# First norm's chain taken first, residual affine passes later, last down projection skewed by 14 rows

## The chip, the core and the metric

One core of one Trainium2 chip runs one launch. The metric is device time in microseconds (us): the median of three runs of the kernel before is 1265.94 us (1265.94 to 1266.82). The profiled execution took 1265.78 us; its span, from the first to the last instruction, is 1264.0 us. TensorE is PE (its weight loads PEld), VectorE is DVE, ScalarE is ACT, SyncE is SP; every load of this kernel is issued from SP's queue.

## The reference

One decoder layer on 256 tokens of width 2048, float32. It mixes tokens (mLSTM and HGRN2 heads, input and output projection), then runs a SwiGLU feed-forward of width 5632. Both sub-layers are modulated by six vectors `mod = silu(c) @ w_mod + b_mod`, and each ends in a residual and a layer norm:

```python
sh1, sc1, g1, sh2, sc2, g2 = jnp.split(mod[:, None, :], N_MOD, axis=-1)
u = x * (1.0 + sc1) + sh1
y = token_mixer(u, ...)                                   # ends with y @ w_out
x = layer_norm(ALPHA * x + (1.0 + g1) * y, ln1_g, ln1_b)  # the first norm
u = x * (1.0 + sc2) + sh2
y = (silu(u @ w_gate) * (u @ w_up)) @ w_down
x = layer_norm(ALPHA * x + (1.0 + g2) * y, ln2_g, ln2_b)  # the second norm
```

## The kernel before

**Split weights.** Each float32 product is made of three matmuls, high by high, high by low and low by high. A weight tile of 128x1024 (512 KB) is loaded by SP into `wr` (4 buffers), ACT copies it to the rounded high half `wh` (5 buffers), DVE subtracts to get the low half `wl` (5 buffers). `w1` (L706) does this, `three` (L718) the matmuls. The 256 tokens are two blocks of 128 rows, t0 and t1, which are the stationary operand; the weights stream past them, 512 columns a matmul.

**Modulation.** Each of 96 vectors `mod(j)` (L170) is a 1 MB load into `m` (2 buffers) and one DVE pass of 128x2048 (L174). Those with j of 48 to 79 (shift and scale of the second sub-layer) are wanted in four groups c, each of four j from 48 on and four from 64 on: `affine1(c)` turns them into the scale and bias columns `sc` with which `make_u2` makes the feed-forward's input `u2` for its k steps 4c to 4c+3. 34 of the 48 modulations of the output projection's stage are spread before it ends; the 14 left (`late`) are asked for by `some(2)` at each k step of the first feed-forward stage.

**Output projection and first norm.** `wo` is taken in two parts over four column groups c. In the last group the matmuls of t0 come first and those of t1 after them (`skew`). `resid` multiplies a bank by the gate (L732) and adds it to the residual `z` (L736), `stat` takes the statistics (L739). Then `norm1(t)`: aggregate (L743), two tiny ACT operations, four passes over z (L810). `turn` transposes z on PE (L817), `make_u2` scales the result on ACT, splits it on ACT and makes the low half on DVE (L838).

**Feed-forward.** `ffn_in((0, 1))` is the first stage: 16 k steps, each with two weight tiles (g = 0 and 1) and both token blocks, 24 matmuls a step. The affine passes that turn the normed z into the residual of the second sub-layer (`affine`, L922 and L923, with the vectors l1g and l1b loaded by `spill`, L847) are asked for in the later stages `up_to`. `down` is the down projection in two passes over four column groups; in the last group of the second pass the last 8 rows (four weight tiles) run first for t0 and then for t1. `finish(t)` is the second norm: statistics, then per quarter L978 and L979 and a store.

**What sets the order.** The program is traced once, and a scheduler orders each engine's instructions by priority, by what it reckons to be ready and by free buffers. `tc.high_priority(n)` raises what is traced inside it, `add_manual_dep` puts one instruction behind another of the same engine without a semaphore. On the chip each engine, and SP's queue, works its list strictly in order.

Of the kernel before, what the change touches and what calls it, by code (L numbers as in the profile page):

```python
# [3 lines left out]
F32 = mybir.dt.float32  # L4
F32R = mybir.dt.float32r
# [32 lines left out]
FIRST = 34  # L38
MIX = (("qk g i", "first"), ("v", "second"), ("o", "p last n"))
NATIVE = ((), ())  # L40
PRI = dict(w=400, e=0, m=-200)

PK = {}
_at = 0
# [35 lines left out]
def build(nc, tc, d):  # L80
    from contextlib import ExitStack

    with ExitStack() as ctx:
# [538 lines left out]
        def mods_some(a):  # L622
            credit[0] += a
            while credit[0] >= 1:
                credit[0] -= 1
                next(modq, 0)
# [77 lines left out]
                act(o[:, 512 * c : 512 * c + 512], bank, AF.Copy)  # L704
            return o

        def w1(src):
            cnt[0] += 1
            r = wr.tile([P, 1024], F32, tag="w", name=f"wr{cnt[0]}")
            nc.sync.dma_start(r, src)  # L710
            h = wh.tile([P, 1024], F32R, tag="h", name=f"wh{cnt[0]}")
            l = wl.tile([P, 1024], F32R, tag="l", name=f"wl{cnt[0]}")
            with tc.high_priority(PRI["w"]):
                act(h, r, AF.Copy)
                tt(l, r, h.bitcast(F32), ALU.subtract)  # L715
            return h, l

        def three(banks, h, l, a, b, first, last):  # L718
# [39 lines left out]
        for part in (1, 0):  # L758
            for c in range(4):
                if part:  # L760
                    banks[c] = [ps(), ps()]
                tiles = []
                skew = part == 0 and c == 3
                for p in range(4):
                    tiles.append(w1(d["wo"][16 * (1 - part) + 4 * c + p]))
                    mods_some(RATE[2])
                    if not skew:
                        for t in range(2):
                            for j in range(2):
                                k = 8 * part + 2 * p + j  # L770
                                w = slice(512 * j, 512 * j + 512)
                                three([banks[c][t]], tiles[-1][0][:, w], tiles[-1][1][:, w], half(yh, k, t), half(yl, k, t), part == 1 and k == 8, part == 0 and k == 7)
                if skew:
                    for t in range(2):
                        for p in range(4):
                            for j in range(2):
                                k = 2 * p + j
                                w = slice(512 * j, 512 * j + 512)
                                three([banks[c][t]], tiles[p][0][:, w], tiles[p][1][:, w], half(yh, k, t), half(yl, k, t), False, k == 7)
                if part == 0:  # L780
                    for t in range(2):
                        resid(t, c, banks[c][t], G1, ALPHA)
                        stat(t, c)
        run(modq)
        late = order2[FIRST:]

        def some(n):
            for _ in range(n):
                if late:
                    run(mod(late.pop(0)))  # L790

        def affine1(c):
            w = slice(4 * c, 4 * c + 4)
            tt(Ac[:, w], pc("l1g", 4 * c, 4), modc[:, 64 + 4 * c : 68 + 4 * c], ALU.mult)
            tt(Bc[:, w], pc("l1b", 4 * c, 4), modc[:, 64 + 4 * c : 68 + 4 * c], ALU.mult)
            tt(Bc[:, w], Bc[:, w], modc[:, 48 + 4 * c : 52 + 4 * c], ALU.add)

        affine1(0)
        affine1(1)
        u2h = [M(name="u2h", dt=F32R) for _ in range(4)]  # L800
        u2l = [M(name="u2l", dt=F32R) for _ in range(4)]

# [3 lines left out]
        def norm1(t):  # L806
            mu, rs = norm(t)
            for c in range(4):
                w = slice(512 * c, 512 * c + 512)
                ts(z[t][:, w], z[t][:, w], mu, rs, ALU.subtract, ALU.mult)  # L810

        zt = {}

        def turn(t, c):
            bank = ps()
            for j in range(4):
                nc.tensor.transpose(bank[:, P * j : P * j + P], z[t][:, 512 * c + P * j : 512 * c + P * j + P], ident)  # L817
            if c < 2:
                zt[t, c] = bank
                return  # L820
            if t == 0:
                zt[c] = M(name="zt")
            zt[t, c] = zt[c][:, 512 * t : 512 * t + 512]
            act(zt[t, c], bank, AF.Copy)

        def make_u2(t, c):
            u = S(512, "s5", bufs=CFG["s5"])
            for j in range(4):
                k = 4 * c + j
                w = slice(P * j, P * j + P)  # L830
                act(u[:, w], zt[t, c][:, w], AF.Identity, scale=Ac[:, k : k + 1], bias=Bc[:, k : k + 1])

            def part(x):
                return x[c].rearrange("p (k t) -> p k t", t=T)[:, :, t * P : t * P + P]
# [9 lines left out]

        def spill(name):
            o = A(name="bc")
            nc.sync.dma_start(o, d[name].broadcast_to([P, D]))  # L847
            return o

        def swi(g, t, gate, up):  # L850
# [28 lines left out]

            return bk, held, block  # L880

        norm1(0)
        for c in range(4):
            turn(0, c)
            if c < 2:
                make_u2(0, c)
        norm1(1)
        use_set(AF.Silu)
        tc.add_manual_dep(table["load"], table["var"].name, order, reason="table")
        bk, held, block = ffn_in((0, 1))  # L890
        for k in range(2):
            for g in range(2):
                held[k, g] = w1(d["wf"][g * KT + k])
            block(k, 0)
        for c in range(4):
            turn(1, c)
            if c < 2:
                make_u2(1, c)
        for k in range(2):
            block(k, 1)  # L900
        for k in range(2, KT):
# [17 lines left out]

        def affine(t, c):  # L920
            w = slice(512 * c, 512 * c + 512)
            stt(z[t][:, w], z[t][:, w], ALPHA, Ag[:, w], ALU.mult, ALU.mult)  # L922
            stt(z[t][:, w], Ab[:, w], ALPHA, z[t][:, w], ALU.mult, ALU.add)  # L923

        mods = list(range(80, 96))
# [20 lines left out]
        def down(k0, k1, G, last):  # L946
            for c in range(4):
                bk = [ps(), ps()]
                held = {}
                skew = 8 if last and c == 3 else 0  # L950

                def pair(k, t):
                    for j in range(2):
                        w = slice(512 * j, 512 * j + 512)
                        three([bk[t]], held[k][0][:, w], held[k][1][:, w], hslice(k + j, t, 0), hslice(k + j, t, 1), k + j == k0, k + j == k1 - 1)

                for k in range(k0, k1, 2):
                    held[k] = w1(d["wd"][22 * c + k // 2])
                    if k < k1 - skew:
                        for t in range(2):  # L960
                            pair(k, t)
                    if k == k0 + 4:
                        while pend:
                            flip(pend.pop(0))
                for t in range(2):
                    for k in range(k1 - skew, k1, 2):
                        pair(k, t)
                    resid(t, c, bk[t], G, None)
                    if last:
                        stat(t, c)  # L970
                        if c == 3:
                            finish(t)

        def finish(t):
            mu, rs = norm(t)
            for c in range(4):
                w = slice(512 * c, 512 * c + 512)
                stt(z[t][:, w], z[t][:, w], mu, Lg[:, w], ALU.subtract, ALU.mult)  # L978
                stt(z[t][:, w], z[t][:, w], rs, Lb[:, w], ALU.mult, ALU.add)  # L979
                nc.sync.dma_start(d["out"][t][:, w], z[t][:, w])  # L980
# [73 lines left out]
```

## Time and profile before

| | |
|---|---|
| median of 3 runs | 1265.94 us |
| profiled execution, its span | 1265.78 us, 1264.0 us |
| PE busy | 1212.8 us, 96% |
| DVE busy | 901.2 us, 71% |
| ACT busy | 591.7 us, 47% |
| DMA | 259 GB/s mean over the span, 285 to 341 GB/s in most slices of the first feed-forward stage |

The page cuts the span into 40 slices of 31.6 us. PE is full in all of them but the first (load and start), the 17th (505.6 to 537.2 us, the first norm, where the granted clock is 0.8 as well) and the last (the second norm). The waits of PE and the timelines of these two places show who was late there.

### The profile page before, as it was taken

Reading aid. Unit: us, or ns where it says so; the run is one execution under the profiler, and the core shown is the slowest. Engines: PE = TensorE matmul, PEld = TensorE weight load, DVE = VectorE, ACT = ScalarE, POOL = GpSimd, SP = SyncE. Lnnn points to the kernel's source line nnn. Section 1 sums busy time; section 2 is a strip of 40 time slices with the busy share of each in tenths; the row PEclk is TensorE's granted clock in tenths of the full one; section 3 lists DMA queues with packets and bytes.
Section 4 is the critical chain, followed back from the end, with each engine's and each line's share of the span. In section 5 each row is a group of like instructions: output and inputs, shape, how many; then the busy total and the mean of one; then the engine's idle time right before and its main releaser. Section 6 shows DMA issues by size and latency. Waiting matters only on the chain.

```text
span 1264.0 us, 17132 instructions
## 1 busy us (share of the span) xinstructions
PE 1212.8 (96%) x6706; PEld 1040.0 (82%) x6706; DVE 901.2 (71%) x979; ACT 591.7 (47%) x743; POOL 3.9 (0%) x13
## 2 busy tenths in 40 slices
PE   4899999999999999799999999999999999999995
PEld 4888899997889887688888888888888888888884
DVE  6778997999999979997877554455555445445655
ACT  4554454835664644644544444433344444434340
POOL 0000000000000000000000000000000000000000
PEclk9999999999999999899999999999999999999998
DMA  9998997857788989889998666666666666676661
GB/s 364 386 335 328 341 398 285 301 200 264 267 327 308 330 317 334 305 320 327 324 329 325 192 190 189 178 194 191 198 191 192 189 194 185 193 256 184 191 191 66
DMA packets 75968, 328.00 MB, mean 260 GB/s; under 512 B 8432, under 2 KB 8816, under 8 KB 62704
## 3 DMA queue, kind: packets, MB, share of 16 engines
q1 hardware_dynamic: 75888, 326.92, 74.9%
q8 instruction: 52, 0.85, 0.3%
q14 instruction: 28, 0.23, 0.0%
HBM read 324.79 MB, written 2.10 MB: 259 GB/s over the span
## 4 chain that ended last, share of the span: by engine, by line
PE 89%; DVE 5%; ACT 3%; issue 2%; DMA 1%; DVEq 0%; ACTq 0%
PE ps L722 21%; PE ps L725 21%; PE ps L721 21%; PE ps L251 5%; PE ps L249 5%; PE ps L250 5%; PE ps L260 2%; PE ps L261 2%; PE ps L262 2%; DVE m L174 2%; PE ps L447 1%; ACT wh L128 1%; DMA m<-in_wmod 1%; DVE wl L213 1%; PE ps L863 1%
## 5 line engine op out<-in xcount | busy, mean ns | idle before, releaser
L128 ACT ACTIVATE wh<-wr 128x1024 fp32r<-128x1024 f32 x408 | 431.1, 1059 | 550.8 <-PE ps L722 426.2
L715 DVE TENSOR_TENSOR wl<-wr,wh 128x1024 fp32r<-128x1024 f32 x296 | 360.6, 1224 | 283.7 <-ACT wh L128 280.4
L721 PE MATMUL ps<-wh,u2h 128*128 128x512 f32 x704 | 275.6, 392 | 0.3 <-ACT s L128 0.3
L722 PE MATMUL ps<-wh,u2l 128*128 128x512 f32 x704 | 273.7, 389 | 0.1
L174 DVE CUSTOM_DVE_ANT_0 m<-m,cb,init 128x2048 f32<-128x2048 f32 x96 | 225.1, 2346 | 22.3 <-DMA m<-in_wmod 22.0
L725 PE MATMUL ps<-wl,u2h 128*128 128x512 f32 x704 | 217.0, 389 | 0.0
L249 PE MATMUL ps<-uh,wh 128*128 128x256 f32 x640 | 184.4, 292 | 22.5 <-ACT wh L128 17.1
L250 PE MATMUL ps<-ul,wh 128*128 128x256 f32 x640 | 181.8, 286 | 0.0
L251 PE MATMUL ps<-uh,wl 128*128 128x256 f32 x640 | 180.3, 287 | 1.1 <-DVE wl L213 1.0
L721 PEld LDWEIGHTS ps<-wh,u2h 128*128 128x128 f32 x704 | 132.6, 188 | 28.9 <-ACT s L128 0.7
L722 PEld LDWEIGHTS ps<-wh,u2l 128*128 128x128 f32 x704 | 132.0, 188 | 28.0 <-DVE u2l L838 0.8
L725 PEld LDWEIGHTS ps<-wl,u2h 128*128 128x128 f32 x704 | 132.1, 188 | 27.6
L213 DVE TENSOR_TENSOR wl<-wr,wh 128x1024 fp32r<-128x1024 f32 x112 | 135.8, 1221 | 25.1 <-ACT wh L128 24.5
L249 PEld LDWEIGHTS ps<-uh,wh 128*128 128x128 f32 x640 | 123.6, 194 | 25.0 <-ACT wh L128 17.8
L721 PE MATMUL ps<-wh,hid 128*128 128x512 f32 x352 | 137.2, 390 | 0.0
L725 PE MATMUL ps<-wl,hid 128*128 128x512 f32 x352 | 137.0, 389 | 0.0
L722 PE MATMUL ps<-wh,hid 128*128 128x512 f32 x352 | 137.0, 389 | 0.0
L250 PEld LDWEIGHTS ps<-ul,wh 128*128 128x128 f32 x640 | 124.5, 195 | 1.3 <-issue 1.0
L251 PEld LDWEIGHTS ps<-uh,wl 128*128 128x128 f32 x640 | 123.2, 194 | 1.9 <-DVE wl L213 1.8
L725 PEld LDWEIGHTS ps<-wl,hid 128*128 128x128 f32 x352 | 66.1, 188 | 13.9
L721 PEld LDWEIGHTS ps<-wh,hid 128*128 128x128 f32 x352 | 66.1, 188 | 13.6
L722 PEld LDWEIGHTS ps<-wh,hid 128*128 128x128 f32 x352 | 66.1, 188 | 13.6
(179 smaller groups left out, 1017.8 us busy)
## 6 DMA issues: line engine op xcount, KB each, us to landing
m<-in_wmod SPq DMA_DIRECT2D x96, 1024.0 KB, 7.1
wr<-in_wf SPq DMA_DIRECT2D x176, 512.0 KB, 4.2
wr<-in_win SPq DMA_DIRECT2D x112, 512.0 KB, 6.0
wr<-in_wd SPq DMA_DIRECT2D x88, 512.0 KB, 3.6
wr<-in_wo SPq DMA_DIRECT2D x32, 512.0 KB, 5.4
xT<-in_x SPq DMA_DIRECT2D x4, 512.0 KB, 8.0
z<-in_xr SPq DMA_DIRECT2D x2, 1024.0 KB, 8.6
out<-z SPq DMA_DIRECT2D x8, 256.0 KB, 2.4
```

The costliest lines, as they stand in the source:

```text
L128: i = nc.scalar.activation(out, in_, f, **kw).ins
L174: table["mod"] = nc.vector.tensor_tensor_reduce(t, t, cb, 1.0, init[:, j : j + 1], ALU.mult, ALU.add, modc[:, j : j + 1]).ins
L213: tt(l[:, :m], r[:, :m], h[:, :m].bitcast(F32), ALU.subtract)
L249: mm(o, h[:, wsl], kt(uh, k0 + k), start=st, stop=False, skip_group_check=True)
L250: mm(o, h[:, wsl], kt(ul, k0 + k), start=False, stop=False, skip_group_check=True)
L251: mm(o, l[:, wsl], kt(uh, k0 + k), start=False, stop=en, skip_group_check=True)
L260: mm(o, a, h[:, w], start=first and k == 0, stop=False, skip_group_check=True)
L261: mm(o, a, l[:, w], start=False, stop=False, skip_group_check=True)
L715: tt(l, r, h.bitcast(F32), ALU.subtract)
L721: mm(o, a, h[:, w], start=first, stop=False, skip_group_check=True)
L722: mm(o, b, h[:, w], start=False, stop=False, skip_group_check=True)
L725: mm(o, a, l[:, w], start=False, stop=last, skip_group_check=True)
```

## The change

Four edits. (1) `resid`, `stat`, `norm1`, `turn`, `make_u2` and `affine1` around the first norm get priorities of 2000 to 3000; weight halves have 400. (2) Manual dependencies put the `late` modulations behind the norm passes of t1 (`normed[1]`), and the low halves of the stage's 2nd to 4th weight tile behind the norm passes of t0 (`normed[0]`). (3) The loads of l1g and l1b, and of l2g and l2b, stand behind the last weight load traced before them, the affine passes behind the low half traced before them. (4) In the last group of the last down pass 14 rows instead of 8 (seven weight tiles) run first for t0 and then for t1; three of the seven live in the pool of `u2`, which is free by then. One modulation step per tile is no longer traced in the last group of the output projection.

```diff
-PRI = dict(w=400, e=0, m=-200)
+PRI = dict(w=400, e=0, m=-200, c=2500)
+SKEW = 14
...
-        def w1(src):
+        def w1(src, spare=False):
...
+            table["load_w"] = nc.sync.dma_start(r, src).ins
+            if spare:
+                h, l = M(name="mh", dt=F32R), M(name="ml", dt=F32R)
...
-                        resid(t, c, banks[c][t], G1, ALPHA)
-                        stat(t, c)
+                        with tc.high_priority(PRI["c"] - 500 * t):
+                            resid(t, c, banks[c][t], G1, ALPHA)
+                            stat(t, c)
...
                     run(mod(late.pop(0)))
+                    after(table["mod"], normed[1])
...
+        def after(i, first):
+            tc.add_manual_dep(i, first.name, order, reason="late")
...
+            i = nc.sync.dma_start(o, d[name].broadcast_to([P, D])).ins
+            after(i, table["load_w"])
...
+        with tc.high_priority(PRI["c"]):
+            norm1(0)
+            for c in range(4):
+                turn(0, c)
+                if c < 2:
+                    make_u2(0, c)
+        normed = [table["norm"]]
+        with tc.high_priority(PRI["c"] - 500):
+            norm1(1)
+        normed.append(table["norm"])
...
                 held[k, g] = w1(d["wf"][g * KT + k])
+                if k or g:
+                    after(table["low"], normed[0])
...
-            stt(z[t][:, w], z[t][:, w], ALPHA, Ag[:, w], ALU.mult, ALU.mult)
+            after(stt(z[t][:, w], z[t][:, w], ALPHA, Ag[:, w], ALU.mult, ALU.mult).ins, table["low"])
...
-                skew = 8 if last and c == 3 else 0
+                skew = SKEW if last and c == 3 else 0
...
-                    held[k] = w1(d["wd"][22 * c + k // 2])
+                    held[k] = w1(d["wd"][22 * c + k // 2], k >= k1 - skew and (k - k1) % 4 == 0)
...
+                    with tc.high_priority(PRI["c"] if last and c == 3 else 0):
+                        resid(t, c, bk[t], G, None)
+                        if last:
+                            stat(t, c)
+                    if last and c == 3:
+                        finish(t)
```

DVE at the first norm, before. Bank ps327 is the last bank of t0, ps328 that of t1; z300 and z301 are the residuals of t0 and t1; wl386 and wl393 are low halves of the feed-forward's weights; m75 is a modulation.

```order
L732 TENSOR_TENSOR s5355_4922<-ps327_4512,bc304_4246 128x512
L715 TENSOR_TENSOR wl386_5040<-wr386_5037,wh386_5039 128x1024
L715 TENSOR_TENSOR wl393_5118<-wr393_5115,wh393_5117 128x1024
L736 SCALAR_TENSOR_TENSOR z300_4240<-z300_4240,s5355_4922 128x512
L732 TENSOR_TENSOR s5356_4926<-ps328_4513,bc304_4246 128x512
L739 BN_STATS st0302_4244<-z300_4240 128x6
L736 SCALAR_TENSOR_TENSOR z301_4241<-z301_4241,s5356_4926 128x512
L743 BN_AGGR mv0365_4944<-st0302_4244 128x2
L174 ISA m75_5235,modc_108<-m75_5235,cb_82,init_100 128x2048
L174 ISA modc_108 128x1
L739 BN_STATS st1303_4245<-z301_4241 128x6
L810 TENSOR_SCALAR z300_4240<-z300_4240,mv0365_4944 128x512 x4
```

And now, from the same operation on, as far as the low half u2l361 of the first input tile:

```order
L736 TENSOR_TENSOR s5355_4922<-ps327_4512,bc304_4246 128x512
L740 SCALAR_TENSOR_TENSOR z300_4240<-z300_4240,s5355_4922 128x512
L743 BN_STATS st0302_4244<-z300_4240 128x6
L747 BN_AGGR mv0365_4944<-st0302_4244 128x2
L818 TENSOR_SCALAR z300_4240<-z300_4240,mv0365_4944 128x512 x4
L719 TENSOR_TENSOR wl384_5016<-wr384_5013,wh384_5015 128x1024
L719 TENSOR_TENSOR wl385_5034<-wr385_5031,wh385_5033 128x1024
L736 TENSOR_TENSOR s5356_4926<-ps328_4513,bc304_4246 128x512
L719 TENSOR_TENSOR wl386_5040<-wr386_5037,wh386_5039 128x1024
L740 SCALAR_TENSOR_TENSOR z301_4241<-z301_4241,s5356_4926 128x512
L719 TENSOR_TENSOR wl393_5118<-wr393_5115,wh393_5117 128x1024
L849 TENSOR_TENSOR u2l361_4940<-s5367_4957,u2h357_4936 128x4x128
```

The norm of t0 moved ahead of everything of t1 and of three of the weights' low halves; no modulation stands in the stretch any more.

PE at the same place, now: the transposes of z300 (L828) with the rows around them. Before, they stood behind all matmuls into ps328.

```order
L726 MATMUL ps328_4513<-wh354_4870,yl299_4223 128x512
L828 MATMUL ps366_4952<-kc_86,z300_4240 128x128 x4
L828 MATMUL ps368_4964<-kc_86,z300_4240 128x128 x4
L828 MATMUL ps370_4976<-kc_86,z300_4240 128x128 x4
L828 MATMUL ps372_4983<-kc_86,z300_4240 128x128 x4
L729 MATMUL ps328_4513<-wl354_4871,yh298_4222 128x512
L725 MATMUL ps328_4513<-wh354_4870,yh298_4222 128x512
L726 MATMUL ps328_4513<-wh354_4870,yl299_4223 128x512
L729 MATMUL ps328_4513<-wl354_4871,yh298_4222 128x512
L725 MATMUL ps375_4999<-wh383_5009,u2h357_4936 128x512
```

Four matmuls of t1's bank moved behind the transposes, and with them the last use of weight tile wh354.

SP's queue in the first feed-forward stage, before: `m` is a modulation of 1 MB, `wr` a weight tile of 512 KB.

```order
L173 DMA m77_5336<-in_wmod 128x2048
L173 DMA m61_5339<-in_wmod 128x2048
L173 DMA m78_5378<-in_wmod 128x2048
L710 DMA wr398_5205<-in_wf 128x1024
L710 DMA wr401_5258<-in_wf 128x1024
L710 DMA wr402_5264<-in_wf 128x1024
L710 DMA wr403_5300<-in_wf 128x1024
L710 DMA wr404_5306<-in_wf 128x1024
L173 DMA m62_5381<-in_wmod 128x2048
L710 DMA wr405_5342<-in_wf 128x1024
L710 DMA wr406_5348<-in_wf 128x1024
L710 DMA wr407_5384<-in_wf 128x1024
```

And now:

```order
L711 DMA wr404_5306<-in_wf 128x1024
L174 DMA m76_5294<-in_wmod 128x2048
L174 DMA m60_5297<-in_wmod 128x2048
L711 DMA wr405_5342<-in_wf 128x1024
L174 DMA m77_5336<-in_wmod 128x2048
L174 DMA m61_5339<-in_wmod 128x2048
L711 DMA wr406_5348<-in_wf 128x1024
L174 DMA m78_5378<-in_wmod 128x2048
L174 DMA m62_5381<-in_wmod 128x2048
L711 DMA wr407_5384<-in_wf 128x1024
L711 DMA wr408_5390<-in_wf 128x1024
```

Six modulations now stand between the weight tiles wr404 and wr407, in pairs, where one stood before. Tiles wr403 and wr404 belong to k step 6, wr405 and wr406 to 7, wr407 and wr408 to 8, wr411 to 9.

## Rows read from the trace of the kernel before

**Rows 1.** The page: span, busy time of PE, share of the chain by engine.

```profile
span 1264.0 us, 17132 instructions
PE 1212.8 (96%) x6706; PEld 1040.0 (82%) x6706; DVE 901.2 (71%) x979; ACT 591.7 (47%) x743; POOL 3.9 (0%) x13
```

**Rows 2.** Waits of PE: who waited for whom, total us, times, longest.

```profile
PE ps L817 <- DVE z L810: 8.2, 1, 8.2
PE ps L494 <- DVE q L478: 3.1, 1, 3.1
```

**Rows 3.** Windows: length, busy us of PE, PEld, DVE, ACT, POOL, granted clock, DMA share, GB/s.

```profile
312.50:313.00 0.50, 0.50 (x6) 0.50 (x6) 0.50 (x2) 0.00 (x0) 0.00 (x0) 0.91 0.94 369
316.00:317.00 1.00, 1.00 (x5) 0.78 (x4) 1.00 (x3) 0.00 (x0) 0.00 (x0) 0.84 1.00 193
...
507.00:508.00 1.00, 0.00 (x0) 0.00 (x0) 1.00 (x3) 0.00 (x0) 0.00 (x0) 0.73 0.79 320
517.00:518.00 1.00, 0.91 (x4) 0.24 (x2) 1.00 (x4) 0.95 (x3) 0.00 (x0) 0.65 0.83 352
```

**Rows 4.** Timeline of PE around the first norm: start, us, instruction, idle before and releaser.

```profile
498.29 0.39 PE L725 MATMUL ps<-wl,yh 128*128 128x512 f32 x1
...
503.73 0.39 PE L725 MATMUL ps<-wl,yh 128*128 128x512 f32 x1
512.28 3.67 PE L817 MATMUL ps<-kc,z 128*128 128x128 f32 x16 [8.17 <-DVE z L810]
...
522.67 1.91 PE L817 MATMUL ps<-kc,z 128*128 128x128 f32 x16
...
532.45 0.39 PE L721 MATMUL ps<-wh,u2h 128*128 128x512 f32 x1
```

**Rows 5.** Timeline of DVE from the first norm to the last of the 14 modulations.

```profile
501.06 2.47 DVE L715 TENSOR_TENSOR wl<-wr,wh 128x1024 fp32r<-128x1024 f32 x2
...
508.12 0.67 DVE L736 SCALAR_TENSOR_TENSOR z<-z,s 128x512 f32<-128x512 f32 x1
508.71 0.25 DVE L743 BATCH_NORM_AGGREGATE mv<-st 128x2 f32<-128x24 f32 x1
508.89 2.28 DVE L174 CUSTOM_DVE_ANT_0 m<-m,cb,init 128x2048 f32<-128x2048 f32 x1
...
511.70 1.89 DVE L810 TENSOR_SCALAR z<-z,mv 128x512 f32<-128x512 f32 x4
...
560.43 2.35 DVE L174 CUSTOM_DVE_ANT_0 m<-m,cb,init 128x2048 f32<-128x2048 f32 x1
```

**Rows 6.** Timeline of ACT around the first norm.

```profile
503.93 1.06 ACT L128 ACTIVATE wh<-wr 128x1024 fp32r<-128x1024 f32 x1 [0.30 <-PE ps L722]
...
509.00 0.29 ACT L128 ACTIVATE mv<-mv,eps 128x1 f32<-128x1 f32 x1 [4.02 <-DVE mv L743]
...
513.43 1.86 ACT L128 ACTIVATE s<-ps,sc 128x128 f32<-128x128 f32 x5 [3.90 <-PE ps L817]
515.16 0.65 ACT L128 ACTIVATE u2h<-s 128x512 fp32r<-128x512 f32 x1
```

**Rows 7.** Modulation loads issued in 515-532, 500-515 and 560-580 us: count, KB, median us to landing.

```profile
m<-in_wmod SPq DMA_DIRECT2D x4, 1024.0 KB, 5.1
...
m<-in_wmod SPq DMA_DIRECT2D x2, 1024.0 KB, 6.4
...
m<-in_wmod SPq DMA_DIRECT2D x2, 1024.0 KB, 8.2
```

**Rows 8.** What SP's queue waited for with a modulation load, whole run.

```profile
SPq L173 <- DVE modc L174: 133.4, 44, 6.0
```

**Rows 9.** Timelines of PE and DVE in the last 20 us.

```profile
1244.58 0.39 PE L725 MATMUL ps<-wl,hid 128*128 128x512 f32 x1
1250.02 0.39 PE L725 MATMUL ps<-wl,hid 128*128 128x512 f32 x1
...
1245.01 0.69 DVE L732 TENSOR_TENSOR s<-ps,bc 128x512 f32<-128x512 f32 x1 [6.07 <-PE ps L725]
1252.79 0.68 DVE L732 TENSOR_TENSOR s<-ps,bc 128x512 f32<-128x512 f32 x1
1259.24 1.41 DVE L979 SCALAR_TENSOR_TENSOR z<-z,mv,bc 128x512 f32<-128x512 f32 x2
```

More of the change, by code (lines that the diff above doesn't have):

```diff
@@ L705, in bcast @@
             return o
-        def w1(src):
+        def w1(src, spare=False):
             cnt[0] += 1
             r = wr.tile([P, 1024], F32, tag="w", name=f"wr{cnt[0]}")
-            nc.sync.dma_start(r, src)
-            h = wh.tile([P, 1024], F32R, tag="h", name=f"wh{cnt[0]}")
-            l = wl.tile([P, 1024], F32R, tag="l", name=f"wl{cnt[0]}")
+            table["load_w"] = nc.sync.dma_start(r, src).ins
+            if spare:
+                h, l = M(name="mh", dt=F32R), M(name="ml", dt=F32R)
+            else:
+                h = wh.tile([P, 1024], F32R, tag="h", name=f"wh{cnt[0]}")
+                l = wl.tile([P, 1024], F32R, tag="l", name=f"wl{cnt[0]}")
             with tc.high_priority(PRI["w"]):
                 act(h, r, AF.Copy)
-                tt(l, r, h.bitcast(F32), ALU.subtract)
+                table["low"] = tt(l, r, h.bitcast(F32), ALU.subtract).ins
             return h, l
@@ L765, in build @@
                     tiles.append(w1(d["wo"][16 * (1 - part) + 4 * c + p]))
-                    mods_some(RATE[2])
+                    if part or c < 3:
+                        mods_some(RATE[2])
                     if not skew:
@@ L796, in affine1 @@
             tt(Bc[:, w], Bc[:, w], modc[:, 48 + 4 * c : 52 + 4 * c], ALU.add)
-        affine1(0)
-        affine1(1)
+        with tc.high_priority(PRI["c"] + 500):
+            affine1(0)
+            affine1(1)
         u2h = [M(name="u2h", dt=F32R) for _ in range(4)]
@@ L809, in norm1 @@
                 w = slice(512 * c, 512 * c + 512)
-                ts(z[t][:, w], z[t][:, w], mu, rs, ALU.subtract, ALU.mult)
+                table["norm"] = ts(z[t][:, w], z[t][:, w], mu, rs, ALU.subtract, ALU.mult).ins
+        def after(i, first):
+            tc.add_manual_dep(i, first.name, order, reason="late")
         zt = {}
@@ L846, in spill @@
             o = A(name="bc")
-            nc.sync.dma_start(o, d[name].broadcast_to([P, D]))
+            i = nc.sync.dma_start(o, d[name].broadcast_to([P, D])).ins
+            after(i, table["load_w"])
             return o
@@ L880, in ffn_in @@
             return bk, held, block
[L882 to L887, printed above, removed]
+        with tc.high_priority(PRI["c"]):
[8 more added lines that the diff above has]
+        normed.append(table["norm"])
         use_set(AF.Silu)
@@ L893, in build @@
                 held[k, g] = w1(d["wf"][g * KT + k])
+                if k or g:
+                    after(table["low"], normed[0])
             block(k, 0)
[L895 to L898, printed above, removed]
+        with tc.high_priority(PRI["c"] - 500):
+            for c in range(4):
+                turn(1, c)
+                if c < 2:
+                    make_u2(1, c)
         for k in range(2):
@@ L967, in down @@
                         pair(k, t)
[L968 to L972, printed above, removed]
+                    with tc.high_priority(PRI["c"] if last and c == 3 else 0):
[4 more added lines that the diff above has]
+                        finish(t)
         def finish(t):
```

## Prediction

> **What bounds the kernel now.** I read the page first: PE is busy 96% of the span, DVE 71% [rows 1], so the time is PE's work plus what PE waits or runs slowly. The table of PE's waits names where: after the start-up (not touched here) one wait is large, 8.2 us for the first norm [rows 2]. The timelines of PE, DVE and ACT around that wait, the windows (for the clock), the answers on loads, and the end of the span came after it.
>
> The loss at the first norm is larger than the wait. PE's last output-projection matmul starts at 503.73, and the work that ends the feed-forward's first two k steps is through when the next matmul starts at 532.45: 28.7 us [rows 4]. A matmul of 512 columns goes every 0.227 us (24 of them from 498.29 to 503.73), a transpose every 0.112 (16 in 1.91) [rows 4]. In those 28.7 us PE issued 54 matmuls and 32 transposes (by the order), 12.3 + 3.6 = 15.9 us at full rate, and the last output matmul's own 0.2. **Lost: 12.6 us.** Part of it is the clock: in 507 to 508 us the granted clock falls from 1.0 to 0.5 (2.4 to 1.2 GHz) and in 517 to 518 it comes back [rows 3].
>
> The reason is DVE. Its operations for t0's bank are spread over 503 to 511.7 between weight low halves, t1's operations and a modulation of 2.28 us, which alone stands between the aggregate at 508.71 and the norm pass at 511.70 [rows 5], although the two ACT operations were ready to follow at 509.00 [rows 6].
>
> **The first norm, worked through.** I walk the new order with these durations: DVE 0.60 us for a 128x512 pass (508.12 to 508.71), 1.14 to 1.24 for a low half, 0.45 to 0.47 for a norm pass (four in 1.89), 2.27 for a modulation [rows 5]; ACT 1.06 for a high half, about 0.5 for the two tiny ones, 2.4 from the first scale operation to the end of the u2 high half (513.43 to 515.81) [rows 6]; a consumer of a bank starts 0.43 after its last matmul starts (1244.58, 1245.01) [rows 9]. t0's bank ends with the matmul at 498.29, so DVE starts at 498.7, and three passes and the aggregate end at 500.9. On ACT the high half of a weight tile now stands between the two tiny operations, and it waits for PE to release its buffer (about 501.2); so the norm passes start at 502.6 and end near 504.4. The transposes run 503.1 to 504.9 at DVE's pace, the four matmuls behind them to 505.85. Only then is wh354 free; ACT's next high half waits for it (505.8 to 506.8, as the one at 503.93 did [rows 6]), and make_u2 stands behind that. u2's high half is there at 506.8 + 2.4 = 509.2: PE waits 3.4 us. DVE goes through four low halves and two passes of t1 before u2's low half: PE waits 0.7 more at 510.1 to 510.8. After that I find nothing late up to the end of the second k step. Lost 4.1 instead of 12.6: **8.5 us gained here.**
>
> **The clock behind it.** A wait of 3.1 us elsewhere, for L494 [rows 2], was followed by a granted clock of 0.91 and 0.84 in the windows at 312.5 and 316 us, with a spell at 0.5 between them [rows 3]: some 3.4 us at half rate, 1.7 us of work. The wait of 3.4 us that is left can bring the same. By DVE's order the second token block's input stands between two modulations, so of the 1.7 us I count 1.2 as passed on to the next part.
>
> The Trainium skill ("TensorE: Matmul & The Clock Gate", HAM oscillation) says that an engine which waits on transfers in each step can be throttled anew in each. That speaks against this change, since the next part makes several waits of 2 to 4 us; three such spells would be 5.1 us instead of my 1.2, and the sum below would be +5.1 instead of +1.2. The trace shows one spell after one wait each; a series of them no row here shows.
>
> **The modulations, which pay for it.** 14 of them (m73 to m63) are late. Before, the last starts at 560.43 [rows 5], five having ended by 515. Now none may start before t1's norm passes, which by the walk end at 514.7. Their data need buffers, of which there are two: a load is issued when the modulation two before it is done (SP waited 133.4 us for this in the run, 44 times [rows 8]). A load alone lands in 5.1 us [rows 7] and the pass takes 2.3: one pair per 7.4 us, as each buffer goes through both. That is slower than PE's step of 5.44 us, and SP's queue is in order: weight tiles stand behind the second load of each pair, which is not issued before the modulation two before it is done.
>
> The walk: m73 514.7, m57 517.5, four low halves, m74 525.0, m58 527.2, m75 534.1, m59 536.4, m76 541.5, m60 545.0, m77 549.0, m61 552.4, m78 556.7, m62 559.8, m79 565.5, m63 568.3. Tile wr406 can be issued when m60 is done and m61's load is out, at 547.7, and lands behind that load near 553.8; its high half is ready at 554.9. PE, going at 5.44 us a step, wants it at 552.5: **2.4 us.** Its low half comes 0.35 late. wr407 is issued at 555.1, ready at 562.3, wanted at 558.0: **4.3 us.** wr411 is issued at 562.5, behind m79 and m63, ready at 570.8, wanted at 567.8: **3.1 us**, and its low half and the next tile 0.7 together. Then all modulations are done and PE runs through. Sum 10.8 us. A slow spell after the wait for wr407 would be eaten by the wait for wr411, which the transfers set. With the 1.2 from above: **12.0 us lost.**
>
> Bounds of this term. Below: if loads cost nothing, DVE alone would still carry two modulations and a low half per half step; the same walk with DVE's durations alone gives waits of 0.4, 0.7, 1.8 and 2.1, together 5.0 us. Above: with loads that share the queue, medians are 6.4 and 8.2 us [rows 7]; at 6.4 each of four pairs takes 1.3 us longer, 5.2 more. I take the value from 5.1, since the first load of a pair has the queue nearly to itself.
>
> The Trainium skill ("DMA: Bandwidth & Descriptors", Queues, rings and completion order) says that an engine takes descriptors in ring order. By that the weight tile issued behind m61 doesn't slow m61, and 5.1 us stands for both loads of a pair: sum +1.2. The row of 8.2 us, where weights were issued around the loads, speaks the other way, and by 6.4 the sum would be +6.4.
>
> **The affine passes and l1g, l1b.** 16 passes of 0.60 us and two loads of 1 MB leave the stretch of 511 to 570 us and go to stages where only weights and modulations of the last vector run. I cost that at nothing: DVE is not full there, and the residual isn't wanted until the down projection. If DVE stalled PE there it would be by one pass, 0.6 us at a time.
>
> **The end.** PE's last matmul starts at 1250.02; its bank could be read at 1250.45, but DVE is at t0's second norm until 1252.79 [rows 9]. With 14 rows t1's matmuls behind t0's bank last 7 x 1.36 = 9.5 us instead of 5.4, and t0's chain takes 1245.01 to 1252.79 = 7.8 us, so it is over 1.3 us before t1's bank ends. **Gain 2.3 us.** Nothing more: t1's own chain from 1252.79 on is unchanged. The cost would be weights: in those 9.5 us a tile is used every 1.36 us, where DVE needs 1.14 to 1.24 each. Three extra buffers and the lead of four tiles that PE's releases leave hide it; if not, the gain is lost, not more.
>
> **Sum.** -8.5 + 12.0 - 2.3 = +1.2 us on the profiled 1265.78; the median shown is 0.16 above it. Forecast 1267.1 us, no change that can be told: a measurement of this kernel can tell about 0.2%, 2.5 us.
>
> **Rivals.** *Slower:* the transfers of a pair share the queue. For it: the 6.4 and 8.2 us rows; against it: 5.1 where modulations were issued one by one. Place: tiles wr406 to wr411, PE's steps 7 to 9; it decides from a pair time of about 8 us on. At 8.7 us, -8.5 + 12.0 + 5.2 - 2.3 = +6.4: 1272.3; half of it 1269.7. *Faster:* the queue holds no tile back, because the weights in their four buffers are further ahead than I walk. For it: before, four modulations in a row were issued without any wait of PE behind 533 us; against it: PE was some 8 us later then. Only DVE's 5.0 and the 1.2 stay: -8.5 + 6.2 - 2.3 = -4.6: 1261.3. *The change does not do what it says:* wh354 and the tile between the two tiny ACT operations keep the first wait near its old 8.2 us; then the gain of 8.5 shrinks by 4.8, and the sum is +6: 1271.9. The order speaks against it, since the norm is three low halves and a modulation shorter.
>
> **Chances.** My forecast with its neighbours, within 0.2%: 0.45. Slower by over 0.2%: 0.33 (sharing 0.27, first norm not shortened 0.06). Faster by over 0.2%: 0.22. The likeliest case alone reaches from 1264.5 to 1268.5; the range takes in most of both sides, 1262.0 to 1271.5.
>
> **What would show it.** Right: PE's wait for L828 gone and one of 3 to 4 us for u2 in its place; modulations of steps 8 to 15 on DVE until about 570 us, in pairs 7 to 8 us apart; PE waits for high halves of `in_wf` tiles between 550 and 575 us, 9 to 12 us together; DVE idle before t1's L736 at the end. Wrong: PE full between 530 and 600 us (then it is faster), pairs 9 us apart (slower), or t1's last chain still queued behind t0's.

## The result, and the profile after

The changed kernel took 1271.45 us (median of 8 runs, 1269.52 to 1276.13), the kernel before 1265.94 us beside it (8 runs). The ratio is 1.0051, 95% interval 1.0037 to 1.0065: 5.5 us slower. Forecast was 1267.1 us and no change that can be told; the sign came out as in the rival "transfers of a pair share the queue" (1269.7 to 1272.3). Every median in this document is of all executions; two single executions of 2470 and 4315 us, in two of the experiments, are left out of the ratios.

The page after, against [rows 1]: the span grew by 3.7 us and PE's busy time by 3.8.

```profile
span 1267.7 us, 17131 instructions
PE 1216.6 (96%) x6706; PEld 1040.7 (82%) x6706; DVE 902.9 (71%) x979; ACT 591.1 (47%) x743; POOL 3.9 (0%) x13
```

PE's waits after, against [rows 2] (who waited for whom, total us, times, longest). The 8.2 us for the norm's passes are gone; in their place stand 3.2 us for u2 and 7.9 us for high halves of weights.

```profile
PE ps L725 <- ACT wh L129: 7.9, 3, 4.4
```

PE's timeline after, against [rows 4] (start, us, instruction, idle before and releaser). 496.81 is the last matmul of t0's bank, 523.98 the first one after the first two k steps, 1255.94 the last of all; the three at 557.59, 565.87 and 573.94 are the first users of tiles wr406, wr407 and wr411.

```profile
496.81 0.39 PE L729 MATMUL ps<-wl,yh 128*128 128x512 f32 x1
...
507.82 1.38 PE L725 MATMUL ps<-wh,u2h 128*128 128x512 f32 x4 [3.17 <-ACT u2h L129]
...
523.98 0.39 PE L725 MATMUL ps<-wh,u2h 128*128 128x512 f32 x1
...
557.59 0.80 PE L725 MATMUL ps<-wh,u2h 128*128 128x512 f32 x1 [4.42 <-ACT wh L129]
...
565.87 0.50 PE L725 MATMUL ps<-wh,u2h 128*128 128x512 f32 x1 [2.80 <-ACT wh L129]
...
573.94 0.50 PE L725 MATMUL ps<-wh,u2h 128*128 128x512 f32 x1 [0.72 <-ACT wh L129]
...
1255.94 0.39 PE L729 MATMUL ps<-wl,hid 128*128 128x512 f32 x1
```

Laid side by side with [rows 4] and [rows 9], these marks cut the difference of 3.7 us into parts:

| stretch | before | after | difference | predicted |
|---|---|---|---|---|
| start to the last matmul of t0's bank | 498.29 | 496.81 | -1.5 | 0 |
| from there to the end of the first two k steps | 34.16 | 27.17 | -7.0 | -8.5 + 1.2 = -7.3 |
| from there to PE's last matmul | 717.57 | 731.96 | +14.4 | +10.8 |
| from there to DVE's last pass | 9.22 | 6.88 | -2.3 | -2.3 |
| rest of the span | 4.76 | 4.88 | +0.1 | 0 |

The first line is no gain of the change. At 312 us the two profiles still agree within 0.1 us: the wait of 3.10 us for q ([rows 2]) ends at 312.27 before and at 312.36 after. Behind it the kernel before ran 3.4 us at half clock ([rows 3]); after, the clock stayed up (window, columns as in [rows 3]):

```profile
313.00:316.00 3.00, 3.00 (x17) 2.52 (x16) 3.00 (x5) 0.66 (x2) 0.00 (x0) 1.00 0.89 358
```

All 13 profiles (before, after and the eleven experiments) have this wait of 3.10 us; eight have the stretch at half clock behind it and five don't, with the old order of the first norm as well as with the new one. So it is luck of the execution. Without these 1.5 us the two spans would differ by 5.2 us, close to the 5.5 of the medians. After's profiled execution was also the shortest of its eight, 1.9 us below its median.

The loss has one place. In windows of 20 us (length, busy us of PE, PEld, DVE, ACT, POOL, granted clock, DMA share, GB/s) PE has 90 records where it is full (a row below, of the kernel without the dependency, shows one); after, these two have 51 and 64:

```profile
543.98:563.98 20.00, 14.50 (x51) 10.63 (x49) 15.73 (x15) 3.25 (x5) 0.00 (x0) 0.83 0.84 316
563.98:583.98 20.00, 17.20 (x64) 12.79 (x65) 17.37 (x19) 12.74 (x19) 0.00 (x0) 0.91 0.90 329
```

65 records are missing, at 0.222 us each: 14.4 us, the whole third line of the table. For 5.5 + 2.8 = 8.3 us of it PE stood still. The granted clock of 0.83 and 0.91 makes another 3.4 + 1.8 = 5.2 us, of which some 0.7 fall into time in which PE stood still anyway; the 1.6 us left are not broken down here. The clock is at its lower level, half rate, in stretches behind the first two of the three waits (windows, same columns):

```profile
558.00:563.00 5.00, 5.00 (x12) 3.40 (x11) 2.78 (x2) 0.00 (x0) 0.00 (x0) 0.50 0.97 370
...
567.00:570.00 3.00, 3.00 (x8) 2.32 (x7) 2.73 (x3) 0.10 (x1) 0.00 (x0) 0.50 1.00 404
```

DVE's late modulations after (m76, m77, m78, m79; the first of all, m73, starts at 513.14), against [rows 5], and its last operations, against [rows 9]:

```profile
544.04 2.35 DVE L175 CUSTOM_DVE_ANT_0 m<-m,cb,init 128x2048 f32<-128x2048 f32 x1 [2.17 <-DMA m<-in_wmod]
...
551.49 2.35 DVE L175 CUSTOM_DVE_ANT_0 m<-m,cb,init 128x2048 f32<-128x2048 f32 x1 [0.48 <-DMA m<-in_wmod]
...
561.01 2.35 DVE L175 CUSTOM_DVE_ANT_0 m<-m,cb,init 128x2048 f32<-128x2048 f32 x1 [2.22 <-DMA m<-in_wmod]
...
568.58 2.35 DVE L175 CUSTOM_DVE_ANT_0 m<-m,cb,init 128x2048 f32<-128x2048 f32 x1 [0.22 <-DMA m<-in_wmod]
...
1256.37 0.69 DVE L736 TENSOR_TENSOR s<-ps,bc 128x512 f32<-128x512 f32 x1 [1.65 <-PE ps L729]
...
1262.82 1.41 DVE L999 SCALAR_TENSOR_TENSOR z<-z,mv,bc 128x512 f32<-128x512 f32 x2
```

DVE waits for the data of m76 and m78 (2.17 and 2.22 us). What the queue did is seen from SP's timeline (start, us over the group, x times):

```profile
529.91 1.26 SPq L711 DMA_DIRECT2D wr<-in_wf  x2
536.88 2.84 SPq L174 DMA_DIRECT2D m<-in_wmod  x2
539.82 0.39 SPq L711 DMA_DIRECT2D wr<-in_wf  x1
546.42 3.80 SPq L174 DMA_DIRECT2D m<-in_wmod  x2
550.32 0.38 SPq L711 DMA_DIRECT2D wr<-in_wf  x1
553.88 4.11 SPq L174 DMA_DIRECT2D m<-in_wmod  x2
558.08 0.86 SPq L711 DMA_DIRECT2D wr<-in_wf  x2
563.40 2.78 SPq L174 DMA_DIRECT2D m<-in_wmod  x2
```

and from the loads' time to landing, issued in 530.6 to 531.2, 536 to 537, 546 to 547, 550.3 to 550.8, 553 to 554, 558.5 to 559 and 563 to 564 us: tile wr404, m76, m77, wr406, m78, wr408, m79.

```profile
wr<-in_wf SPq DMA_DIRECT2D x1, 512.0 KB, 8.7
...
m<-in_wmod SPq DMA_DIRECT2D x1, 1024.0 KB, 7.1
...
m<-in_wmod SPq DMA_DIRECT2D x1, 1024.0 KB, 4.9
...
wr<-in_wf SPq DMA_DIRECT2D x1, 512.0 KB, 6.1
...
m<-in_wmod SPq DMA_DIRECT2D x1, 1024.0 KB, 7.0
...
wr<-in_wf SPq DMA_DIRECT2D x1, 512.0 KB, 7.4
...
m<-in_wmod SPq DMA_DIRECT2D x1, 1024.0 KB, 5.0
```

When m76 was issued (536.9), wr404 had some 2.5 us to go (530.6 + 8.7 = 539.3); when m78 was issued (553.9), wr406 had 2.5 (550.3 + 6.1 = 556.4). Both landed 4.5 to 4.7 us behind the tile ahead. But a tile ahead doesn't by itself make a load slow: when m79 was issued (563.4), wr408 had 2.5 us to go too (558.5 + 7.4 = 565.9), and m79 took 5.0. m77 took 4.9 with wr405 due 1.3 us after its issue.

What sets m76 and m78 apart is their end. Each load here closes with 16 packets of a few bytes (the page counts 8432 packets under 512 B for 527 transfers). Of m78's, 15 came in 558 to 559.5 us and the last one only in 560 to 561 (DMA, these two windows); of m76's, 14 had come by 542.6 and the last two at 543.6. Why these parts were late is not shown.

```profile
DMA packets 69, 0.44 MB, mean 295 GB/s; under 512 B 15, under 2 KB 15, under 8 KB 15
...
DMA packets 51, 0.41 MB, mean 410 GB/s; under 512 B 1, under 2 KB 1, under 8 KB 1
```

### The profile page after: what moved, and what is told of

The parts are those of the page before. It is cut to its first block, busy times and chain, and to the rows that moved or that the text cites. A ratio compares the mean times of both kernels' runs of the same rounds, so it can differ in the third digit from the quotient of the medians.

```text
span 1267.7 us, 17131 instructions
## 1 busy us (share of the span) xinstructions
PE 1216.6 (96%) x6706; PEld 1040.7 (82%) x6706; DVE 902.9 (71%) x979; ACT 591.1 (47%) x743; POOL 3.9 (0%) x13
## 2 busy tenths in 40 slices
DMA packets 75968, 328.00 MB, mean 259 GB/s; under 512 B 8432, under 2 KB 8816, under 8 KB 62704
## 4 chain that ended last, share of the span: by engine, by line
PE 85%; DVE 6%; DMA 4%; ACT 3%; issue 2%; DVEq 0%; ACTq 0%
PE ps L726 20%; PE ps L729 20%; PE ps L725 20%; PE ps L252 5%; PE ps L250 5%; PE ps L251 5%; DMA m<-in_wmod 4%; DVE m L175 3%; PE ps L261 2%; PE ps L262 2%; PE ps L263 2%; PE ps L448 1%; ACT wh L129 1%; DVE wl L214 1%; PE ps L875 1%
## 5 line engine op out<-in xcount | busy, mean ns | idle before, releaser
L725 PE MATMUL ps<-wh,hid 128*128 128x512 f32 x340 | 132.5, 390 | 0.0
L729 PE MATMUL ps<-wl,hid 128*128 128x512 f32 x340 | 132.3, 389 | 0.0
L726 PE MATMUL ps<-wh,hid 128*128 128x512 f32 x340 | 132.3, 389 | 0.0
L725 PEld LDWEIGHTS ps<-wh,hid 128*128 128x128 f32 x340 | 63.8, 188 | 13.3
L726 PEld LDWEIGHTS ps<-wh,hid 128*128 128x128 f32 x340 | 63.8, 188 | 13.2
```

The source lines that it names most:

```text
L725: mm(o, a, h[:, w], start=first, stop=False, skip_group_check=True)
L726: mm(o, b, h[:, w], start=False, stop=False, skip_group_check=True)
L729: mm(o, a, l[:, w], start=False, stop=last, skip_group_check=True)
```

## Experiments

The theory: the dependency that puts the late modulations behind t1's norm costs all of the loss, because two `m` buffers and an in-order queue hold weight tiles back. Rivals: DVE's passes alone do it; the moved affine passes or the tail cost something; the half-clock stretches come on top of the waits.

**The dependency taken away.**

```diff
                     run(mod(late.pop(0)))
-                    after(table["mod"], normed[1])
```

> The changed kernel without the one dependency that puts the 14 late modulations behind the second norm's passes; all else stays (priorities of the first norm, late affine passes, skew of 14 rows). Theory (the dependency costs it: the modulations come late, in pairs that SP's in-order queue puts ahead of weight tiles): by the new order the modulations run before and right behind the norm as in the kernel before, so the waits for high halves of 4.42, 2.80 and 0.72 us and the half-clock stretches behind them go, while a modulation between t0's aggregate and its norm passes costs some 2 to 3.5 us: 1256 to 1261 us, faster than both kernels. Rival (the late affine passes, the l1g and l1b loads or the tail cost the time): at most 3 us off, 1268 to 1272.

Measured: 1256.09 us, ratio to before 0.9921 (0.9909 to 0.9934). The waits for high halves are gone and PE is full where 65 records were missing. At the first norm two modulations stand between t0's bank and its norm passes, with a wait of 3.2 us (PE's waits, then a window):

```profile
PE ps L827 <- DVE z L817: 3.2, 1, 3.2
```
```profile
543.98:563.98 20.00, 20.00 (x90) 16.57 (x89) 16.17 (x18) 5.80 (x8) 0.00 (x0) 1.00 0.90 337
```

As the theory had it. Everything else in the change together is worth 9.6 us; this one line cost about 15.

**Tail and affine passes alone; affine passes alone.** The kernel before with edits (3) and (4), and the same with `SKEW = 8` (the raised priority of the last chain stays in both).

> The kernel before with only the affine passes and the l1g, l1b, l2g, l2b loads put behind weights and the skew of 14 rows with its raised last chain; no priorities and no dependencies around the first norm or the modulations. Theory: the affine move costs nothing and the tail gives 2.3 us: 1263.6 us (1262.5 to 1265). Rival (affine passes or the moved loads cost in the later stages): 1266 or more, with waits of PE behind 580 us. In both the first norm keeps its 8 us wait.

> The kernel before with only the affine passes and the loads of l1g, l1b, l2g, l2b put behind weights; skew of 8 rows. Theory (the move costs nothing and gains nothing): 1265 to 1266.5 us, as the kernel before; the difference of 1.2 us between the 3.6 measured for both moves and the 2.3 read at the tail was start-up drift. Rival (16 passes of 0.6 us and 2 MB less beside the first feed-forward stage gain some 1 us): 1264 to 1265. Rival (the passes cost in the later stages): over 1267.

Measured: both edits 1262.17 us, 0.9966 (0.9954 to 0.9979); affine alone 1265.41 us, 0.9987 (0.9976 to 0.9999). The affine move costs nothing and may gain 1 us or so; the difference of the two ratios, 0.0021, is 2.7 us for the tail, uncertain by some 2 us by their intervals. With both edits, the tail's row is that of the changed kernel: t1's chain starts after DVE was idle for 1.65 us, 0.43 us behind the start of PE's last matmul at 1253.76, so that t0's chain is no longer in its way (timeline of DVE).

```profile
1254.19 0.69 DVE L736 TENSOR_TENSOR s<-ps,bc 128x512 f32<-128x512 f32 x1 [1.65 <-PE ps L729]
```

**Passes without loads, loads without passes, more buffers.** Three changes to the late modulations of the changed kernel, the dependency kept: no load; a product over 64 columns only; every second tile in the big pool.

```diff
-            nc.sync.dma_start(t, d["wmod"][j])
+            if not still:
+                nc.sync.dma_start(t, d["wmod"][j])
...
-            table["mod"] = nc.vector.tensor_tensor_reduce(t, t, cb, 1.0, ...
+            table["mod"] = nc.vector.tensor_tensor_reduce(t, cb if still else t, cb, 1.0, ...
```

```diff
-            table["mod"] = nc.vector.tensor_tensor_reduce(t, t, cb, 1.0, ...
+            table["mod"] = nc.vector.tensor_tensor_reduce(t[:, :n], t[:, :n], cb[:, :n], 1.0, ...
```

```diff
-            t = mr.tile([P, D], F32, tag="m", name=f"m{j}")
+            t = big.tile([P, D], F32, tag="a", name=f"n{j}") if spare else mr.tile([P, D], F32, tag="m", name=f"m{j}")
```

> The changed kernel, but the 14 late modulations load nothing: their passes run on a tile that is already on the chip (the computation leaves out 14 of the 96 products of the modulation). DVE keeps its 14 passes of 2.3 us behind the norm; SP's queue and the m buffers no longer hold weight tiles back. Theory (transfers through two buffers and the in-order queue): the waits for high halves go, 10 to 14 us less than the changed kernel, 1257 to 1262 us. Rival (DVE's passes and low halves alone make PE wait): 5 us of waits and spells at half clock stay, 1264 to 1269.

> The changed kernel, but the 14 late modulations take their product over 64 of 2048 columns only (the computation leaves out the rest of these 14): the loads of 1 MB stay, behind the same dependency and through the same two buffers, and DVE's passes shrink from 2.3 us to about 0.1. The reverse of the kernel that kept the passes and dropped the loads. Theory (transfers: two loads and two weight tiles in turn on one queue need 8.5 to 9.5 us a pair, whatever DVE does): waits for high halves of 2 to 3 us each at three tiles stay, 3 to 5 us less than the changed kernel, 1266 to 1268 us. Rival (the time of a pair is load plus pass, so without the pass a pair takes 5 to 6 us and PE's step of 5.44 us hides it): no waits in steps 7 to 10, 1259 to 1263 us.

> The changed kernel with every second late modulation in a buffer of the big pool instead of the two m buffers, so that its load is issued ahead; the dependency behind the second norm stays. Theory (two buffers gate the loads, and these the weight tiles): waits at tiles wr406 to wr411 shrink to under 3 us in all, a wait near wr417 may remain (by the new order some 3 to 4 us), 1260 to 1266 us. Rival (DVE's passes after the norm are the limit): 5 us and more of waits stay, 1266 to 1270. Rival (the loads share the queue, whatever the buffers): as the changed kernel, 1270 to 1272.

Measured: without loads 1262.70 us, 0.9972 (0.9961 to 0.9982); without passes 1260.45 us, 0.9949 (0.9935 to 0.9962); with more buffers 1262.57 us, 0.9969 (0.9958 to 0.9980). Each takes 9 to 11 us off the changed kernel, and no two of these gains can be added. That fits a loss which neither the loads nor the passes make by themselves, but both in turn through two buffers. It is not a clean proof: in each of the three the scheduler also put SP's and DVE's other work in a new order.

Without loads the time lies between the two expectations (1257 to 1262 and 1264 to 1269), and no high half is late. DVE's passes end so late that u2 of the last group c is: PE's timeline, steps 12 on.

```profile
581.25 1.19 PE L726 MATMUL ps<-wh,u2h 128*128 128x512 f32 x4 [1.41 <-ACT u2h L129]
583.45 2.08 PE L726 MATMUL ps<-wh,u2h 128*128 128x512 f32 x4 [1.01 <-ACT u2h L129]
```

With more buffers it is the same place, one wait of 3.00 us:

```profile
583.55 1.82 PE L725 MATMUL ps<-wh,u2h 128*128 128x512 f32 x4 [3.00 <-ACT u2h L129]
```

Without passes the waits for high halves stay, but short, 1.31 and 1.72 us, and the window ahead of them (the last two columns are the DMA share and GB/s) shows the queue full:

```profile
530.00:556.00 26.00, 26.00 (x117) 21.52 (x116) 11.48 (x26) 10.60 (x16) 0.00 (x0) 1.00 1.01 395
```
```profile
558.53 0.50 PE L725 MATMUL ps<-wh,u2h 128*128 128x512 f32 x1 [1.31 <-ACT wh L129]
...
566.38 0.50 PE L725 MATMUL ps<-wh,u2h 128*128 128x512 f32 x1 [1.72 <-ACT wh L129]
```

My expectation for this one was wrong by 6 us, and the time lies in the rival's range: waits stayed, as the theory said, but were half as long, and the pairs started 7.7 us apart (523.17 to 553.97 in four steps), neither 8.5 to 9.5 nor 5 to 6. In the same window, 530 to 556 us, the changed kernel moved 308 GB/s, this one 395. I read the difference as slots in which a load waits for a buffer that DVE still reads. But SP's order changed too: two weight tiles stand between the pairs here, where the changed kernel has one, and no run separates the two.

**Zeros into the waits.** Matmuls that add zeros keep PE at work in a wait; does the time fall when the half-clock stretch behind it goes? First ahead of three tiles (the `FILL` shown), then 4 against 24 of them ahead of wr406 alone (`{(7, 1): 4}` and `{(7, 1): 24}`), where the orders of PE, DVE, ACT and SP are the same in both.

```diff
+FILL = {(7, 1): 24, (8, 0): 34, (9, 0): 22}
...
+                    for _ in range(FILL.get((k, g), 0) if t == 0 and gs == (0, 1) else 0):
+                        mm(bk[g, t, 0][:, 0:256], zero, kr, start=False, stop=False, skip_group_check=True)
```

> The changed kernel with 24, 34 and 22 matmuls of 256 columns that add zeros to a bank (stationary operand all zero, the result is unchanged), in PE's order just ahead of the three tiles wr406, wr407 and wr411 that it waits for, so that PE works through most of each wait instead of standing still; some 9.6 us of work at 0.12 us each in place of 10.8 us of waits. Theory A (transfers set when the three tiles come, so the half-clock stretch behind one wait is paid by the next): the stretches at half clock go, but the time stays as that of the changed kernel, 1269.5 to 1272 us. Theory B (the stretches of 2.7 and 1.6 us come on top of the waits): 1266 to 1268 us. If the filling is too long for the waits: slower than the changed kernel.

> The changed kernel with 4 matmuls of 256 columns that add zeros ahead of tile wr406 alone (0.5 us of PE's first large wait, which is 4.4 us without them). Each engine's order is the same as in the kernel with 24 of them, so the two differ in nothing but how long PE stands still there. Both theories: PE waits near 4 us, a stretch at half clock follows, 1270 to 1272.5 us.

> The same with 24 such matmuls ahead of tile wr406 (2.7 to 2.9 us of work in a wait of 4.4 us, the rest below 2 us). The half-clock stretch behind this wait goes. Theory A (the next tiles come when the transfers let them, so a stretch is paid out of the next wait): the same time as with 4, within 1 us, and the wait for wr407 longer by what the stretch took, some 2.5 us. Theory B (the stretch comes on top): 2.5 us less than with 4.

Measured: three tiles 1273.83 us, 1.0063 (1.0050 to 1.0075), which decides nothing: the third filling came after its tile was there (22 matmuls, 2.76 us), and the order on SP and DVE had moved. With 4: 1271.32 us, 1.0041 (1.0027 to 1.0055). With 24: 1273.05 us, 1.0052 (1.0031 to 1.0073). PE at wr406, wr407 and wr411, with 4 and then with 24:

```profile
554.94 0.50 PE L726 MATMUL ps<-wh,u2h 128*128 128x512 f32 x1 [2.76 <-ACT wh L130]
...
564.04 0.79 PE L726 MATMUL ps<-wh,u2h 128*128 128x512 f32 x1 [4.49 <-ACT wh L130]
...
574.68 0.50 PE L726 MATMUL ps<-wh,u2h 128*128 128x512 f32 x1 [2.50 <-ACT wh L130]
```
```profile
559.43 0.50 PE L726 MATMUL ps<-wh,u2h 128*128 128x512 f32 x1 [1.30 <-ACT wh L130]
...
568.30 0.80 PE L726 MATMUL ps<-wh,u2h 128*128 128x512 f32 x1 [5.84 <-ACT wh L130]
...
577.43 0.50 PE L726 MATMUL ps<-wh,u2h 128*128 128x512 f32 x1 [1.72 <-ACT wh L130]
```

Windows behind wr406, with 4 and with 24, and one behind wr411 with 4 (the granted clock is the third column from the right):

```profile
555.00:558.00 3.00, 3.00 (x8) 2.36 (x9) 1.15 (x1) 0.00 (x0) 0.00 (x0) 0.60 1.01 303
```
```profile
559.00:562.00 3.00, 2.57 (x11) 2.13 (x12) 1.63 (x3) 0.38 (x1) 0.00 (x0) 1.00 0.94 358
```
```profile
576.20:579.20 3.00, 3.00 (x8) 2.39 (x8) 1.99 (x2) 3.00 (x6) 0.00 (x0) 0.50 0.69 194
```

With 24 the stretch at half clock behind wr406 is gone. PE comes to its wait for wr407 3.03 us after wr406's first matmul instead of 4.61 (568.30 - 5.84 - 559.43 and 564.04 - 4.49 - 554.94), 1.58 us sooner, and then waits 1.35 us longer (2.5 expected): wr407 comes 8.87 us after wr406 instead of 9.10. For this stretch theory A holds in this pair of profiles: what PE loses behind one wait it would have waited at the next.

For a stretch behind the last wait it doesn't. With 4 one stands behind wr411, with 24 none, and from wr411's first matmul to PE's last (1257.29 and 1258.74) it is 682.6 us with 4 and 681.3 with 24: 1.3 us that no later wait takes back, in this one pair of profiles. The kernel with 24 isn't faster by its times, but these can't weigh 1 or 2 us: the intervals overlap, and the two profiled executions are 3.8 us apart before the first norm already (t0's first transpose at 500.50 and 504.26).

**A version that beats both.** The first four late modulations free, the other ten behind t0's norm; then the same with 8 rows of skew.

```diff
-                    after(table["mod"], normed[1])
+                    if len(late) < 10:
+                        after(table["mod"], normed[0])
```

> The changed kernel, but of the 14 late modulations only the last ten carry the dependency, and it puts them behind the norm passes of t0 instead of t1; the first four are free and run before the last bank of t0 is complete, as in the kernel before. Theory: no modulation stands between t0's bank and its norm passes (the kernel without the dependency had two there and a wait of 3.2 us with a stretch at half clock behind it), and ten late ones fit beside the low halves: waits of at most 1 us at the first norm, none in steps 7 to 10: 1252 to 1255 us, faster than all so far. Rival (ten behind the norm still gate the weight tiles through the two buffers): waits of 2 us and more at 545 to 565 us, 1257 or more.

> The kernel with ten late modulations behind t0's norm, with a skew of 8 rows instead of 14. Theory (the tail's gain doesn't depend on the rest): 2.3 us more than with 14 rows, 1257 to 1258.5 us, t1's last chain queued behind t0's passes again. Rival (the skew gives nothing once the rest is faster): 1255 to 1256.

Measured: 1255.40 us, 0.9910 (0.9895 to 0.9925), just above the expected range, and with a skew of 8 1257.00 us, 0.9922 (0.9908 to 0.9935). By the medians the first is 16 us below the changed kernel; from the kernel without the dependency it can't be told apart. One modulation did stand between t0's bank and its norm, against my expectation, but the waits are short, 0.6 us for z and 1.1 for u2, and the clock stays at 1.0 behind them (PE's waits, then a window):

```profile
PE ps L725 <- ACT u2h L129: 1.1, 1, 1.1
```
```profile
508.00:514.00 6.00, 4.90 (x23) 3.63 (x22) 6.00 (x9) 4.89 (x13) 0.00 (x0) 1.00 0.41 108
```

The skew's 1.6 us by the medians is below the predicted 2.3, with intervals that overlap.

## Why the prediction was wrong

**The first norm: right.** Norm passes 4.3 us behind t0's bank (501.09 - 496.81; predicted 502.6 - 498.29), ACT's high half held by wh354 as walked, a wait of 3.17 instead of 3.4 for u2 and 0.2 instead of 0.7 for its low half, a half-clock stretch behind it. 7.0 us gained where 7.3 were forecast.

**The tail and the affine passes: right,** 2.3 us by the rows and nothing.

**The modulations: the mechanism was right, and the step that failed is the duration of a load.** The prediction put it so: "I take the value from 5.1, since the first load of a pair has the queue nearly to itself." In two of the four pairs it didn't come out: m76 took 7.1 and m78 7.0 us where 5.1 was walked (m77 4.9, m79 5.0), and every later load and tile moved with them. Tiles wr406, wr407 and wr411 were walked as ready at 554.9, 562.3 and 570.8; PE got on at 557.59, 565.87 and 573.94, 2.7, 3.6 and 3.1 us later. 10.8 + 3.1 = 13.9 of the 14.4 us. The upper bound that I had written down (6.4 us a load, four pairs, 5.2 us more) held it, and the rival built on it decides "from a pair time of about 8 us on": SP's pairs started 9.5, 7.5 and 9.5 us apart (536.88, 546.42, 553.88, 563.40). What made these two loads longer stays open. A weight tile let go by the pair before was ahead of both, but m79 had as much of a tile ahead of it as m78 and took 5.0; what came late in m76 and m78 were the last of their 16 closing packets.

The Trainium skill ("DMA: Bandwidth & Descriptors", Queues, rings and completion order) has descriptors taken in ring order. The trace agrees as far as order goes: wr404, m76, m77, wr406 and m78 landed at 539.3, 544.0, 551.3, 556.4 and 560.9, in the order of their issue. The order gives no price, though. I concluded from it that a tile behind a load doesn't slow it, and walked both loads of a pair with 5.1 us, where the first ones measured 4.9 to 7.1.

**The half-clock stretches: right as far as it was tried.** "A slow spell after the wait for wr407 would be eaten by the wait for wr411" is what the pair of 4 and 24 matmuls shows for the stretch one tile earlier; for the one behind wr407 it wasn't tried. The Trainium skill's sentence ("TensorE: Matmul & The Clock Gate", HAM oscillation) that each wait on transfers can throttle anew holds here: a stretch at 0.50 behind two of the three waits in a row. My sum from it, +5.1, lies close to the measured +5.5 by luck: it adds the stretches to the waits, and the one that was tried lay inside time that the transfers had taken already, while the waits themselves were longer than walked. The row from which I took the price of a stretch, the one behind the wait of 3.1 us, was itself a matter of the execution: eight profiles of 13 have it.

**The first norm's price.** I saw that the modulations paid for it and took the two edits as one. They are two: without the dependency the priorities, and the low halves held behind t0's norm, still give the difference between 0.9921 and the 0.9966 of tail and affine passes, some 6 us.

## What to carry to other kernels

Work that is pushed behind a milestone doesn't only run later: its loads, its buffers and the queue behind them move with it, and an in-order queue passes the delay on to loads that have nothing to do with it. When a chain of buffer, load and pass is walked, don't give each load the time of one that ran alone: here loads of one size in one stretch took 4.9 to 7.1 us, and the walk has to hold for the longest of them as well. A stretch at low clock, or any delay, behind a wait costs only if the next thing waited for doesn't come later anyway; behind the last wait one cost 1.3 us here. And before a difference between two profiles is read as a gain, look for a stretch at low clock that only one of them has.

## What the runs showed of the hardware

- Loads of 1 MB in one stretch landed in 4.9, 5.0, 7.0 and 7.1 us. The two long ones waited for the last one or two of their 16 closing packets; some 2.5 us of a weight tile still ahead went with 7.1 us, with 7.0 and with 5.0.
- In 530 to 556 us the queue moved 395 GB/s in the kernel whose passes were nearly nothing, and 308 in the changed kernel.
- PE's single waits of 1.10, 1.30, 1.31 and 1.72 us had no fall of the granted clock behind them; those of 2.50, 2.76, 2.80, 3.00, 3.17, 4.42 and 4.49 had one to 0.5. The wait of 3.10 us for q, the same in all 13 profiles, had one in eight of them and none in five. Two waits of 1.41 and 1.01 us, 2.2 us apart, had one too (window of that kernel without loads):

```profile
580.00:590.00 10.00, 7.20 (x17) 4.96 (x18) 8.11 (x8) 3.36 (x7) 0.00 (x0) 0.66 0.91 355
```
